# Stores and loads of split queries and latents on ScalarE's queue, and shorter due times for the mixers' steps

## The chip, the core and the metric

The kernel runs on one core of a Trainium2 chip. A core has TensorE (PE in the profile; its weight loads are the row PEld), VectorE (DVE), ScalarE (ACT), GpSimd (POOL) and SyncE (SP). Each engine runs its own list of instructions in order and waits at semaphores for the others. DMAs are begun by an engine's queue and carried out by 16 DMA engines. The metric is the time of one execution in microseconds (us).

## What is computed

One inference step of a two-layer decoder trunk, float32, over 1024 prompt tokens and 8 x 4 sampled tokens (1056 columns in all). Each layer projects its normalised input once (`x @ w_in`) and feeds three groups of heads: SSD (a Mamba-2 mixer, 16 heads of 64), MLA (latent attention, 8 heads, key/value latent 256, query rank 384, rotary keys of 32) and GDN (gated DeltaNet, 4 heads of 128). Their outputs are gated, joined and projected back, and a LayerNorm closes the layer. The sampled tokens' attention also reads 8192 cached positions through a page table. Cut to what matters here:

```python
proj = x @ w_in                                  # feeds SSD, MLA and GDN
y_ssd = rms_norm(ssd_scan(...) * silu(z))
cq  = rms_norm(mla_cq, mla_q_norm_w)             # 384 wide: the query latents
ckv = rms_norm(mla_ckv, mla_kv_norm_w)           # 256 wide: key/value latents, also an output
q = cq @ mla_w_uq                                # 8 heads x (64 + 32); the 32 are rotated
o_lat = mla_attention(q_lat, q_rope, [past, ckv], [past_rope, kr], pos)
y_gdn = rms_norm(gdn_scan(...)) * silu(z)
x = layer_norm(ALPHA * x + [y_ssd | y_mla | y_gdn] @ w_out)
```

## The kernel before

Everything lies transposed: channels on the 128 partitions, tokens along the free dimension, in three blocks of 384, 384 and 288 columns (`BLOCKS`). A float32 operand of a big product is split into a high part in a type that TensorE reads at full rate and a low part (the rest); `mm3` makes a product from high x high, high x low and low x high. `split` (L160 to L166) makes the high part with a ScalarE copy and the low part with a subtraction on GpSimd, or on VectorE where the call says so.

Each layer has two phases. In phase 1 (`phase1`) the order of TensorE's instructions is written out by `merge` (L372), a planner with a clock of its own. The clock advances by what each matmul ought to take. There are three threads of work:

- `fill`: the 46 chunks of the input projection (`proj`, three blocks each), then, when the input's tiles are given back, the queries (`mla_q`: 18 products, 6 chunks in 3 blocks), then, after stream a has ended (`yield {"a"}`), the keys and values (`mla_kv`: 16 products) with the decode queries (`absorb`) in their midst.
- stream a: `misc`, GDN heads 0 and 2, `mla_in` (it norms the key/value and query latents, splits them and stores the halves to `ckd` and `cqd` in HBM), SSD group 0.
- stream b: the first LayerNorm, GDN heads 1 and 3, `gdn_sample`, SSD group 1.

A stream's step ends in `yield t`: its next step is due when the clock has passed `t` more microseconds, and until then `fill` goes on. `yield {…}` waits until the named chunks or stages are done. The order so made is TensorE's; the other engines' and queues' orders are made by the framework's scheduler from its own estimates. The steps that the change touches:

- `rstd` (L305): column sums on TensorE, then a power of -1/2 on VectorE and GpSimd (L317, L318), `yield 5.5`, then the broadcast on TensorE. It serves `mla_in` (6 a layer), `ssd_norm` (3 for each SSD group), the first LayerNorm (three blocks in layer 0, one in layer 1), and phase 2's LayerNorms, where `finish` goes through it without waiting for due times.
- `gdn_block` (L858), two halves for each head: after the norm of its output, `yield 7.5`, then the transposes back (L150).
- `ssd` (L1031): three groups of transposes and score products, `yield 2.5` between them.
- `ssd_sample` (L1212): at a group's end, `rstd` for two prompt blocks, then eight updates of sampled states, the first due after 7.0, the others after 2.03, then the sampled y (stored to `yd`), and `ssd_norm` of the last block, which reads it back, scales it and stores it to `mixd`.

All plain DMAs are begun by SP's queue, which keeps its order (`dma`, L134 to L136, takes another engine as its last argument). Four kinds of them bear on the change: `mla_in`'s stores of halves (30 a layer, tiles `c` or `q` to `ckd`, `cqd`); `latents` (six loads `cq` from `cqd`, two for each block); `store` in `mla_q` (36 stores `qd` from `stage`); and in `absorb` eight loads of decode queries (`c` from `qxd`). The tiles `cq` lie where the input's tiles lay, those of the first block among them.

Phase 2 begins with `decode_units`: 32 units, each of which gathers cached rows with GpSimd's indirect DMAs (`dec_v`, `dec`) into room that lay in phase 1's tiles (b's region `p_b` first, then the projection's weights), transposes them on VectorE and multiplies them (`ps_dS`, `ps_dV`). The prompt's attention is woven in, then the output projection. In the profile's names, `ps_pj`, `ps_a` and `ps_b` are PSUM banks of the projection, stream a and stream b (the queries, keys and values use `ps_pj` and `ps_a` by turns); `c` and `q` are a's regions, `p_b` and `p_sb` are b's.

Of the kernel before, what the change touches and what calls it, by code (L numbers as in the profile page):

```python
# [127 lines left out]
class Builder:  # L128
# [177 lines left out]
    def rstd(self, T, tag, ss, n, mul, eps, soon=contextlib.nullcontext):  # L306

        nc = self.nc
        ws = [(j, c, min(128, n - c)) for j, c in enumerate(range(0, n, 128))]
        ps, r = self.psum(tag), T(8)  # L310
        for j, c, w in ws:
            self.mm(ps[:w, j:j + 1], lhsT=ss[:, c:c + w], rhs=self.ones[:, 0:1], start=True, stop=True)
        full = n // 128
        with soon():
            for p, u in ((128, slice(0, full)), (n % 128, slice(full, full + 1))):
                if p:
                    nc.vector.tensor_scalar(out=r[:p, u], in0=ps[:p, u], scalar1=mul, scalar2=eps, op0=ALU.mult, op1=ALU.add)  # L317
                    nc.gpsimd.tensor_tensor(out=r[:p, u], in0=r[:p, u], in1=self.mhalf[:p, 0:1].to_broadcast([p, u.stop - u.start]), op=ALU.pow)  # L318
        yield 5.5
        ps = self.psum(tag)  # L320
        for j, c, w in ws:
            self.mm(ps[:, c:c + w], lhsT=r[:w, j:j + 1].to_broadcast([w, 128]), rhs=self.ident[:w, :w], start=True, stop=True)
        return ps[:, :n]
# [385 lines left out]
    def gdn_block(self, r, L, T, Q, h, nb, x, S, ahead):  # L709
        nc = self.nc  # L710
        k, q, v, zs, g, bt = x
# [143 lines left out]
        ro = norm(po, 1.0 / 128, RMS_EPS)  # L855
        on = t(T)
        self.tt(nc.vector, v3(on), v3(po), bc(ro))
        yield 7.5  # L858
        p = tps(on)
        self.stt(on, p, self.gnwh[:, 0:1], zs)  # L860
        self.mix_out(12 + h, c0, n, on)
# [157 lines left out]
    def ssd(self, r, g):  # L1019
        nc, l = self.nc, self.l  # L1020
        R = Ring(self.reg[r][0])
        yield {-1, 17 + g * 10, 18 + g * 10}
        CT, Bt, CB, acc = R(NT), R(9 * 128), R(8 * 128 + 32), R(NT)
        X, X2 = R.rest(), Ring(self.reg[r][1])
        BT = X(NT)
        self.dma(BT, self.pd[:, 16 + g * 2])
        self.dma(CT, self.pd[:, 17 + g * 2])
        yield 13.0
        for t0 in (0, 4, 8):
            if t0:  # L1030
                yield 2.5  # L1031
            p, p2 = self.psum(r), self.psum(r)
            for t in range(t0, min(t0 + 4, 9)):
                w = 128 if t < 8 else 32
                o = (t - t0) * 128
                self.tp(p[:w, o:o + 128], BT[:, t * 128:t * 128 + w])
                self.mm(p2[:w, o:o + w], lhsT=BT[:, t * 128:t * 128 + w], rhs=CT[:, t * 128:t * 128 + w], start=True, stop=True)
            with self.tc.high_priority():
                if t0 < 8:
                    nc.scalar.copy(out=Bt[:, t0 * 128:t0 * 128 + 512], in_=p)  # L1040
                    self.tt(nc.vector, CB[:, t0 * 128:t0 * 128 + 512].rearrange("p (c n) -> p c n", c=4), p2.rearrange("p (c n) -> p c n", c=4),
                            self.const[:, C_INC:C_INC + 128].unsqueeze(1).to_broadcast([128, 4, 128]))
                else:
                    nc.scalar.copy(out=Bt[:32, 1024:1152], in_=p[:32, :128])
                    self.tt(nc.vector, CB[:32, 1024:1056], p2[:32, :32], self.const[:32, C_INCS:C_INCS + 32])

        big = self.sm(r, F32R)
        K = slice(0, 96)
        bs = X(128)
        self.stack(bs.bitcast(F32R), Bt[0:32, 1024:1152], 1)  # L1050
        self.tt(nc.gpsimd, big[K, 512:1536].rearrange("p (b n) -> p b n", b=8), bs[K].unsqueeze(1).to_broadcast([96, 8, 128]),
                self.const[K, C_BMT:C_BMT + 8].unsqueeze(2).to_broadcast([96, 8, 128]))
        for k in range(4):
            yield {19 + g * 10 + 2 * k, 20 + g * 10 + 2 * k}
            Y = Ring(X.a, X.base, X.size)
            yield from self.ssd_pair(r, Ring(Y(3 * 512)), Ring(X2.a), Ring(Y(6 * 128)), g * 4 + k, CT, Bt, CB, acc, k == 0)
        yield from self.ssd_sample(r, X, X2, g, CT, Bt, CB, acc, big)
# [95 lines left out]
    def ssd_sample(self, r, X, T, g, CT, Bt, CB, acc, big):  # L1153
# [55 lines left out]
        for b in range(8):  # L1209
            if b == 4:  # L1210
                old((6, 7))
            yield 2.03 if b else 7.0  # L1212
            p = self.psum(r)
            self.mm(p, lhsT=b3[K, b], rhs=xs[K], start=True, stop=True)
            self.tt(nc.vector, hb[b], hb[b], p, ALU.add)
            self.dma(self.o["ssd_s"][l, :, g, b], hb[b])
# [23 lines left out]
    def mla_in(self, r):  # L1240
        nc, l = self.nc, self.l
        par = self.par[l]
        a, b = self.reg[r]
        R = itertools.cycle([(Ring(a, 0, 1920), Ring(a, 1920, 2304)), (Ring(a, 4224, 1920), Ring(b))])
        yield set(range(37, 42))
        for first, cnt, pn, dst in ((39, 2, P_KVN, self.ckd), (36, 3, P_QN, self.cqd)):
            for nb, (c0, n, _) in enumerate(BLOCKS):
                T, T2 = next(R)
                raw = T(cnt * 384)[:, :cnt * n].rearrange("p (c n) -> p c n", c=cnt)
                self.dma(raw, self.pd[:, first:first + cnt, c0:c0 + n])  # L1250
                acc, sq = T(384)[:, :n], T(384)[:, :n]
                for c in range(cnt):
                    self.act(sq if c else acc, raw[:, c], AF.Square)
                    if c:
                        self.tt(nc.gpsimd, acc, acc, sq, ALU.add)
                yield 6.61
                sq = yield from self.rstd(T2, r, acc, n, 1.0 / (128 * cnt), RMS_EPS)
                for c in range(cnt):
                    self.stt(raw[:, c], raw[:, c], par[:, pn + c:pn + c + 1], sq)
                    hi, lo = (T2(384)[:, :n].bitcast(F32R) for _ in range(2))  # L1260
                    self.split(None, raw[:, c], n, hi, lo)
                    self.dma(dst[0][:, c, c0:c0 + n], hi)
                    self.dma(dst[1][:, c, c0:c0 + n], lo)
                if cnt == 2:
                    self.dma(self.o["ckvT"][l, :, :, c0:c0 + n], raw)
                    if nb == 2:
                        self.dma(self.cks, raw[:, :, 256:288])
        self.done.add("latents")

    def mla_q(self, cq, rot, ck, T):  # L1270
# [8 lines left out]
        def latents(nb):  # L1279
            c0, n, _ = BLOCKS[nb]  # L1280
            for k in range(2):
                self.dma(cq[nb][:, k], self.cqd[k][:, :, c0:c0 + n])

        banks = itertools.cycle(("pj", "a"))

# [8 lines left out]
        def store(c, nb, *q):  # L1294
            c0, n, _ = BLOCKS[nb]
            for d, a in zip(self.qd, q):
                self.dma(d[c * 128:c * 128 + 128, c0:c0 + n], a)

        def table(nb, *places):
            c0, n, _ = BLOCKS[nb]  # L1300
# [91 lines left out]
    def absorb(self):  # L1392
# [22 lines left out]
        for g in range(4):  # L1415
            G = slice(g * 32, g * 32 + 32)
            for r in range(2):
                self.dma(qx[G, r * 4:r * 4 + 4], self.qxd[:, r].rearrange("(s a) n -> a s n", s=4))
            self.dma(self.cso[G, 384:640], self.qxr)


# [608 lines left out]
```

## Time and profile before

| | |
|---|---|
| median of 3 runs | 3480.68 us (3480.07 to 3483.55) |
| the profiled execution | 3483.24 us, of which its span 3481.4 |
| TensorE busy | 3091.7 us (89% of the span), 33880 matmuls |
| VectorE busy | 2216.9 us (64%) |
| ScalarE busy | 1325.7 us (38%) |
| GpSimd busy | 1176.1 us (34%) |
| DMA | 564.70 MB in 317070 packets, mean 162 GB/s |
| phase 1, first layer | 0 to about 1051 us |
| phase 2, first layer | to about 1762 us |
| phase 1, second layer | to about 2757 us |

A row of the timeline has the start, the length, the engine, the line, the operation and its tiles (out<-in), its shape and count; in brackets stands how long the engine was idle before it and what ended that. Matmuls are pipelined and their ends modelled, so a busy TensorE isn't TensorE at its peak. A share of the whole span is a mean over stages with different limits, so the stages are read one by one.

### The profile page before, as it was taken

The numbers are of one execution on the slowest core, as the hardware profiler recorded it, in microseconds if no ns is written. First come the engines' busy times: TensorE is split into PE (matmuls) and PEld (weight loads), VectorE is DVE, ScalarE is ACT, GpSimd is POOL, SyncE is SP. The second block draws the span as 40 slices with busy tenths as digits, with TensorE's granted clock in tenths as the row PEclk, the third lists the DMA queues.
The fourth block names the chain that finished last, engine by engine and source line by source line (L and its number), as shares of the span: only waits on it lengthen the run. The fifth ranks groups of instructions, "written<-read, shape, count | busy, mean of one in ns | idle before, by whom it ended". The sixth has DMA issues, their size and how long they took to land. (4 is left out here: it accounts for less than half of the span.)

```text
span 3481.4 us, 82579 instructions
## 1 busy us (share of the span) xinstructions
PE 3091.7 (89%) x33880; PEld 2621.0 (75%) x33880; DVE 2216.9 (64%) x4610; ACT 1325.7 (38%) x3099; POOL 1176.1 (34%) x1250
## 2 busy tenths in 40 slices
PE   5899999898777888899988999989897788888997
PEld 4889998798664555569978999888886555555797
DVE  6767366577555666655687663756876456667456
ACT  4433333343222333354543332443332233334544
POOL 3444434755432212120143444455454212112100
PEclk7999999899888999999999999999998899999999
DMA  3332323556876655535434232255669656554354
GB/s 127 122 102 88 106 73 124 166 180 196 275 240 221 203 184 190 183 126 187 161 103 128 92 97 94 69 168 161 185 211 326 215 179 209 193 186 161 118 204 136
DMA packets 317070, 564.70 MB, mean 162 GB/s; under 512 B 51772, under 2 KB 218748, under 8 KB 299668
## 3 DMA queue, kind: packets, MB, share of 16 engines
q1 hardware_dynamic: 293140, 408.42, 37.1%
q0 software_dynamic: 23552, 151.01, 12.0%
q8 instruction: 266, 4.36, 0.5%
q14 instruction: 112, 0.92, 0.1%
HBM read 429.00 MB, written 130.30 MB: 161 GB/s over the span
## 5 line engine op out<-in xcount | busy, mean ns | idle before, releaser
L180 PE MATMUL ps_pj<-xh,w_r 128*128 128x384 f32 (+1 forms) x4416 | 1205.7, 340 | 65.3 <-DVE p_cv L156 29.4
L180 PEld LDWEIGHTS ps_pj<-xh,w_r 128*128 128x128 f32 x4416 | 809.7, 194 | 83.9 <-DVE p_cv L156 33.3
L180 PE MATMUL ps_pj<-xl,w_r 128*128 128x384 f32 (+1 forms) x2208 | 731.9, 331 | 5.5 <-POOL xl L153 5.4
L180 PEld LDWEIGHTS ps_pj<-xl,w_r 128*128 128x128 f32 x2208 | 429.0, 194 | 15.6 <-POOL xl L153 14.0
L156 DVE SCALAR_TENSOR_TENSOR p_cv<-p_cv,c 128x384 f32<-128x384 f32 (+1 forms) x432 | 359.5, 834 | 63.7 <-ACT p_cv L159 57.2
L180 PE MATMUL ps_dS<-dec_k,c 32*32 32x256 f32 x8192 | 332.1, 383 | 18.4 <-DVE dec_k L1704 2.1
L153 POOL TENSOR_TENSOR w_r<-w_raw,w_r 128x1024 fp32r<-128x1024 f32 (+1 forms) x98 | 235.1, 2400 | 242.8 <-ACT w_r L165 220.4
L180 PEld LDWEIGHTS ps_dS<-dec_k,c 32*32 32x32 f32 x8192 | 184.5, 106 | 144.6 <-issue 104.4
L1704 DVE STREAM_TRANSPOSE dec_k<-dec_v 128x2048 f32<-128x2048 f32 x128 | 291.0, 2281 | 0.0
L1680 POOL DMA_INDIRECT dec<-cache_k_rope,c x64 | 60.7, 949 | 523.7 <-DVE dec L1773 521.2
L159 ACT ACTIVATE c<-ps_aS,c 128x512 f32<-128x512 f32 (+3 forms) x192 | 111.2, 579 | 215.7 <-DVE c L1559 214.5
L159 ACT ACTIVATE p_cv<-p_cv 128x384 f32<-128x384 f32 x144 | 72.4, 503 | 302.7 <-DVE p_cv L156 302.2
L1680 POOL DMA_INDIRECT dec_v<-cache_kv_latent,c x128 | 120.3, 940 | 183.8 <-PE ps_dV L180 122.9
L180 PE MATMUL ps_b<-p_b 128*128 128x128 f32 (+7 forms) x1476 | 154.2, 285 | 10.5 <-DVE p_b L156 3.7
L180 PE MATMUL ps_dV<-dec_v,dec 128*32 128x256 f32 x2048 | 129.5, 395 | 37.5 <-ACT dec L1740 34.8
L180 PE MATMUL ps_aS<-mix,wo 128*128 128x384 f32 (+1 forms) x960 | 159.6, 322 | 1.4 <-DVE wo L153 1.4
L1558 DVE TENSOR_REDUCE c<-ps_aS 128x1 f32<-128x512 f32 (+3 forms) x192 | 105.3, 548 | 84.0 <-PE ps_aS L180 81.2
L1717 DVE TENSOR_REDUCE dec<-ps_dS 128x1 f32<-128x512 f32 x64 | 44.2, 691 | 179.6 <-PE ps_dS L180 179.5
L153 DVE TENSOR_TENSOR wo<-c,wo 128x1024 fp32r<-128x1024 f32 x92 | 115.4, 1254 | 67.0 <-ACT wo L165 66.6
L1515 ACT COPY c<-ps_aT 128x512 f32<-128x512 f32 (+3 forms) x192 | 89.9, 478 | 177.6 <-PE ps_aT L150 157.2
L180 PEld LDWEIGHTS ps_aS<-mix,wo 128*128 128x128 f32 x960 | 152.1, 188 | 3.6 <-DVE wo L153 2.3
L165 ACT CAST wo<-c 128x1024 fp32r<-128x1024 f32 x96 | 100.5, 1047 | 141.3 <-PE ps_aS L180 70.6
(348 smaller groups left out, 6007.3 us busy)
## 6 DMA issues: line engine op xcount, KB each, us to landing
c<-w_out SPq DMA_DIRECT2D x96, 512.0 KB
w_raw<-w_in SPq DMA_DIRECT2D x92, 512.0 KB
pd<-p_cv SPq DMA_DIRECT2D x164, 192.0 KB
p_b<-pd SPq DMA_DIRECT2D x66, 256.0 KB
c<-pd SPq DMA_DIRECT2D x64, 256.0 KB
q<-rowd SPq DMA_DIRECT2D x48, 256.0 KB
p_b<-rowd SPq DMA_DIRECT2D x48, 256.0 KB
pd<-p_cv SPq DMA_DIRECT2D x82, 144.0 KB
```

Of the source, the lines that this page charges most:

```text
L153: eng.tensor_tensor(out=out, in0=a, in1=b, op=op)
L156: self.nc.vector.scalar_tensor_tensor(out=out, in0=a, scalar=s, in1=b, op0=op0, op1=op1)
L159: self.nc.scalar.activation(out=out, in_=in_, func=func, **kw)
L165: self.nc.scalar.copy(out=hi, in_=src)
L180: return self.nc.tensor.matmul(out, lhsT=lhsT, rhs=rhs, start=start, stop=stop)
L1515: nc.scalar.copy(out=t[:, :w], in_=p[:, :w])
L1558: nc.vector.reduce_max(out=m, in_=ps[:, :w], axis=AX.X)
L1680: nc.gpsimd.indirect_dma_start(out=out, out_offset=None, in_=src, in_offset=bass.IndirectOffsetOnAxis(ap=idx[:, c:c + 1], axis=0))
L1704: nc.vector.transpose(T[r].rearrange("p j s k -> p j (s k)"), V[:, :, r * 128:r * 128 + 128])
L1717: nc.vector.tensor_reduce(out=al, in_=s3, axis=AX.XY, op=ALU.max)
```

## The change

Five due times are shortened (`rstd` 5.5 to 4.0, the end of a GDN half 7.5 to 5.5, SSD's first groups 2.5 to 1.6, the sampled states 7.0 to 4.5 and 2.03 to 1.5), and four kinds of DMA are begun by ScalarE's queue: all of `mla_in`'s split halves, of the latents' loads and of the split queries' stores, and every second pair of the decode queries' loads. No instruction is added or taken away.

```diff
@@ rstd
-        yield 5.5
+        yield 4.0
         ps = self.psum(tag)
@@ gdn_block
         self.tt(nc.vector, v3(on), v3(po), bc(ro))
-        yield 7.5
+        yield 5.5
         p = tps(on)
@@ ssd
             if t0:
-                yield 2.5
+                yield 1.6
             p, p2 = self.psum(r), self.psum(r)
@@ ssd_sample
-            yield 2.03 if b else 7.0
+            yield 1.5 if b else 4.5
             p = self.psum(r)
@@ mla_in
                     self.split(None, raw[:, c], n, hi, lo)
-                    self.dma(dst[0][:, c, c0:c0 + n], hi)
-                    self.dma(dst[1][:, c, c0:c0 + n], lo)
+                    self.dma(dst[0][:, c, c0:c0 + n], hi, nc.scalar)
+                    self.dma(dst[1][:, c, c0:c0 + n], lo, nc.scalar)
@@ mla_q, latents
             for k in range(2):
-                self.dma(cq[nb][:, k], self.cqd[k][:, :, c0:c0 + n])
+                self.dma(cq[nb][:, k], self.cqd[k][:, :, c0:c0 + n], nc.scalar)
@@ mla_q, store
             for d, a in zip(self.qd, q):
-                self.dma(d[c * 128:c * 128 + 128, c0:c0 + n], a)
+                self.dma(d[c * 128:c * 128 + 128, c0:c0 + n], a, nc.scalar)
@@ absorb
             for r in range(2):
-                self.dma(qx[G, r * 4:r * 4 + 4], self.qxd[:, r].rearrange("(s a) n -> a s n", s=4))
+                self.dma(qx[G, r * 4:r * 4 + 4], self.qxd[:, r].rearrange("(s a) n -> a s n", s=4), nc.scalar if g % 2 else nc.sync)
```

## Rows read from the trace of the kernel before

**Rows 1.** The page's first line.

```profile
span 3481.4 us, 82579 instructions
```

**Rows 2.** Windows: stretch, length, busy us of five engines, TensorE's clock, DMA share, GB/s.

```profile
570.00:921.00 351.00, 318.97 (x2307) 301.81 (x2306) 230.79 (x520) 125.42 (x266) 195.71 (x192) 0.95 0.61 188
921.00:1051.00 130.00, 87.55 (x476) 71.12 (x484) 67.97 (x142) 34.69 (x71) 45.79 (x52) 0.82 0.83 276
...
2625.00:2757.00 132.00, 89.79 (x484) 73.02 (x484) 68.39 (x138) 33.46 (x69) 46.81 (x52) 0.81 0.80 269
```

**Rows 3.** Timeline, TensorE, from the last projection to the first query products.

```profile
920.32 0.29 PE L180 MATMUL ps_pj<-xh,w_r 128*128 128x288 f32 x1
931.79 0.58 PE L180 MATMUL ps_pj<-cq,w_r 128*128 128x288 f32 x1 [11.19 <-DMA cq<-cqd]
934.34 2.29 PE L180 MATMUL ps_pj<-cq,w_r 128*128 128x288 f32 x8 [1.97 <-DMA cq<-cqd]
```

**Rows 4.** Timeline, SP's queue, at the first load of latents.

```profile
925.12 0.38 SPq L136 DMA_DIRECT2D mixd<-q  x1
925.59 0.58 SPq L136 DMA_DIRECT2D cq<-cqd  x1
```

**Rows 5.** Timeline, ScalarE, at the end of the projections.

```profile
911.52 0.49 ACT L159 ACTIVATE p_cv<-ps_pj 128x384 f32<-128x384 f32 x1 [6.77 <-PE ps_pj L180]
...
920.30 0.63 ACT L159 ACTIVATE p_b<-p_b 128x512 f32<-128x512 f32 x1 [6.57 <-DVE p_b L1108]
```

**Rows 6.** Timeline, TensorE, from the last query product to the first decode product.

```profile
980.04 3.07 PE L180 MATMUL ps_a<-cq,w_r 128*128 128x384 f32 x9 [2.64 <-DVE q L153]
...
990.70 0.27 PE L180 MATMUL ps_a<-c,c 128*32 128x1 f32 x2 [3.14 <-DVE c L1234]
992.12 0.76 PE L180 MATMUL ps_b<-p_sb 96*128 96x512 f32 x1 [1.15 <-DVE p_sb L153]
992.68 1.62 PE L180 MATMUL ps_a<-c,c 128*128 128x128 f32 x6
...
1030.15 0.65 PE L180 MATMUL ps_b<-c,p_b 128*128 128x1 f32 x6
...
1050.63 1.11 PE L180 MATMUL ps_dS<-dec,c 32*32 32x256 f32 x16 [17.69 <-issue]
```

**Rows 7.** The chain of waits, end of the second layer's phase 1: start, length, what.

```profile
2731.46 2.09 PE ps_b L180 x24
...
2735.16 1.39 PE ps_a L180 x6
...
2737.23 4.03 DMA p_b<-yd
...
2743.30 1.82 DMA mixd<-p_b
...
2748.60 6.79 DMA dec<-cache_k_rope,c
```

**Rows 8.** Timeline, TensorE: four steps behind due times that the change shortens.

```profile
318.57 1.47 PE L150 MATMUL ps_b<-c,p_b 128*128 128x128 f32 x12
...
361.59 0.60 PE L150 MATMUL ps_a<-c,q 128*128 128x128 f32 x4
...
580.29 0.83 PE L180 MATMUL ps_a<-c,c 128*128 128x128 f32 x6
...
734.30 0.49 PE L180 MATMUL ps_b<-p_b 128*128 128x128 f32 x2 [1.64 <-ACT p_b L1040]
```

**Rows 9.** Timeline, VectorE and GpSimd: what the first three steps need.

```profile
316.75 0.68 DVE L153 TENSOR_TENSOR p_b<-ps_b,p_sb 128x512 f32<-128x512 f32 x1
...
355.05 0.69 DVE L153 TENSOR_TENSOR q<-ps_a,p_sa 128x512 f32<-128x512 f32 x1
...
574.60 0.86 POOL L318 TENSOR_TENSOR c<-c,c 128x3 f32<-128x3 f32 x1
```

**Rows 10.** Waits of SP's queue, 921 to 1051: waiter, releaser, us, times, longest.

```profile
SPq L136 <- DVE stage L153: 5.3, 5, 3.8
```

**Rows 11.** The split queries by tile: issues, ns min/median/max, first and last start.

```profile
L136 SPq DMA_DIRECT2D qd<-stage x72: 319/403/2110, 945.0 to 2696.5; - x72
```

## The prediction

> **What bounds the kernel now.** I read the table of windows first, because a share over the whole span [rows 1] hides the stages. While the projections run, TensorE is the bound or close to it (319.0 of 351 us busy). In the stage behind them, from the last projection to the first decode product, it is busy for 87.6 of 130 us at a granted clock of 0.82, and the second layer repeats this: 89.8 of 132 us at 0.81 [rows 2]. Those two stretches are where time lies open, 42 us in each layer. Nothing in the change touches phase 2 itself: `rstd` runs there too, but `finish` throws its delays away.
>
> I then read TensorE's timeline of that stage for the rows that begin with a wait. They fall in three clusters.
>
> First, right behind the last projection (920.6) TensorE waits 11.19 us for the first half of the split query latents, and 1.97 us more for the second [rows 3]. The reader should ask why that load is late, not how long it takes. It goes into the room of the input's first block. ScalarE evacuates that block's last bank from 911.52 on [rows 5], so the input tiles below it are free then. The load is issued at 925.59, 14 us later, in SP's order behind a mixer's store that waited for VectorE [rows 4]. It lands 6.2 us after its issue, when TensorE starts at 931.79.
>
> Second, the queries' products end at 983.1 (980.04 and 3.07 us), but `fill` may not go on to keys and values before stream a has ended. So a's last steps stand alone in the order and TensorE waits for them: 2.64 us (a bank that a's state update still held), 3.14 and 1.15 us, 6.9 in all. The products that may follow begin when a's last `rstd` is through [rows 6].
>
> Third, the products of keys and values end by 1030.15, where b's last norm begins, and the first decode product comes at 1050.63, 20.5 us later [rows 6]. The chain of waits in the second layer says what that is: stream b's step that makes its last y ends at 2733.55; y is stored, read back for the norm (4.03 us), scaled, stored to the mix (1.82 us), and only then does b's region come free for the gathers of the cache, of which the key part lands at 2755.39 [rows 7]. That is 21.8 us of latency behind b's step, 18.8 behind the last product of keys and values (2736.55).
>
> **The change part by part.** Two things are changed: due times in the planner that orders TensorE, and the queue of 76 DMAs in each layer.
>
> *Due times.* Shorter ones move no work away. They move a stream's step forward in an order that the projections fill. For stream b the steps ahead of its last y lose 4 x 2.0 (GDN halves) + 2 x 0.9 (SSD's start) + 2 x 1.5 (norms) + 2.5 + 7 x 0.53 (sampled states) = 19.0 us of due time. For stream a the sampled part alone loses 9.2 + 1.5 = 10.7, and the steps ahead of it 6 x 1.5 + 8.0 + 1.8 = 18.8, of which some is lost again because its pairs wait for their projections.
>
> - Second cluster: a ends at 994.3 (992.68 and 1.62 us), and must end 11.2 us earlier, at 983.1, to be out of the way. 10.7 and a part of 18.8 suffice, so a's steps lie under products and the 6.9 us go. Ends: 3 (a bank wait stays) and 6.9. I take 6.9.
> - Third cluster: b's step now ends 3.0 us ahead of the last product of keys and values [rows 7]. It moves forward by 19.0, while those products move forward by the 6.9 just counted, so by some 12 against them, and it ends 15 us ahead. The key part would land 21.8 - 15 = 6.8 us after them in place of 18.8, a gain of 12; I take 11, since due times are the planner's microseconds and not the chip's. What is late next is the same chain, shorter. Ends: 0 (the gathers wait for something else of the old region) and 18.8.
> - What it may cost: a step due before its operands are ready stalls TensorE, which keeps its order, and every projection behind it. `rstd`: GpSimd is ready at 575.46, the product comes at 580.29, 4.8 us of room for 1.5. A GDN half: VectorE ready at 355.74, transposes at 361.59, 5.9 us for 2.0; the tightest has 317.43 to 318.57, 1.1 for 2.0, so 0.9 lost [rows 8, 9]. SSD's start already waits 1.64 us for a bank in stream b [rows 8]; two steps there come 0.9 sooner, so 1.8 lost. The sampled states: nothing, up to the rival below. Sum 2.7 a layer; ends 0 and 5.
>
> *Queue.* The 30 stores of split latents and 36 of split queries, six loads of latents and four of the decode queries leave SP. What stays on SP behind them (weights, rows, states) waits for fewer strangers; I cost that at nothing, as none of the three clusters waits for such a load.
>
> - The latents' loads: on ScalarE's queue they no longer stand behind b's store, but ScalarE keeps order too. In this trace an exponential blocks it from 913.7 (the end of the one before) to 920.30 [rows 5]. Ahead of that, the load goes out at 912 and TensorE waits for nothing (gain 13.2, the sum of the two waits). Behind it, it goes out at about 921, lands at 927 and gains 4.6 and most of the second wait, 6. Behind everything, 0. I take 7: with b's steps earlier the exponential stands elsewhere, and I can't tell where.
> - The stores: each now costs ScalarE an issue, 0.40 us in the median as SP's rows have it and 2.11 at most [rows 11], and a wait for the low part. On SP, waits for VectorE's low parts were 5.3 us in this stage, 3.8 the longest [rows 10]. Behind a waiting store on ScalarE stand casts that empty PSUM banks, and behind those TensorE. With about half its time idle here (34.7 of 130 us busy [rows 2]) I let half of the 5.3 reach TensorE: 2.7 a layer. Ends: below nothing by the SP relief, say -2, and 40 (below).
> - The decode queries' loads: four of eight elsewhere; nothing, they end before the decode's start as it will be.
>
> The page "DMA: Bandwidth & Descriptors" of the Trainium skill, section "Issuing engines are not separate DMA queues", speaks against this half: it says that starting DMAs from several engines saves only the sequencer's time to start them. Here a row shows a load that could have gone 14 us earlier and was held by the order of its queue, which is more than an issue; by the page's rule the loads' term is 0 and the time is that of the first rival.
>
> **Sum.** A layer: 7 + 6.9 + 11 - 2.7 - 2.7 = 19.5 us, two layers 39. The profiled execution took 3483.2 (span 3481.4), the median is 3480.7 (3480.1 to 3483.6), so the sum is 3444.2 on the profiled one and **3442** as a median. I add nothing for a clock that falls less after shorter waits; if it comes, it is a gain.
>
> **The rivals.**
>
> - *The queue is worth nothing*: the loads wait on ScalarE as long as on SP. For it: ScalarE also keeps order, and its exponential waits for a row load of SP's. Against: the tiles are free at 911.5. Net 6.9 + 11 - 2.7 - 2.7 = 12.5 a layer: 3456.
> - *All three clusters close*: 13.2 + 6.9 + 18.8 - 2.7 = 36.2 a layer: 3408. Against it: the chain of rows 7 doesn't get shorter itself.
> - *New waits of TensorE take it back*: some 40 steps a layer are due earlier (8 GDN halves, 12 norms, 4 SSD starts, 16 states). At 0.5 us of wait for each, 20 us, the gain is gone: about 3481. For it: the rows at 318.57 and 734.30; against it: the rooms of 4.8 and 5.9.
> - *Slower: ScalarE becomes the bound of the query stage.* Place: 18 products with two stores each, from 931.8 to 983.1, one in 2.85 us. ScalarE needs a cast, 0.49 by the nearest row of that size [rows 5], and two issues, 0.81; it has 1.55 us left for the wait of each product. Beyond that point each product is late. If each waited the 3.8 us that SP's longest took, 18 x 2.25 = 40 us a layer: 22.2 - 40 = -18 a layer, 3517. For it: nothing else empties those banks; against it: five such waits in the stage, 1.1 us in the mean [rows 10].
>
> **How the numbers follow.** Forecast 0.45 (3430 to 3455); queue worth nothing 0.2; all close 0.1; new waits 0.13, of which 0.08 lies within 0.2%; slower 0.12. 0.2% is 7 us, about what a measurement of this kernel can tell from no change. Faster 0.80, same 0.08, slower 0.12. The range takes in the first two, most of the third and the nearer part of the fourth: 3410 to 3478.
>
> **What would show it.** After: the latents' loads issued by ScalarE, TensorE's wait behind the last projection 2 to 7 us and not 13; no wait between the last query product and the first of keys and values, with a's last norm ahead of them; the first decode product 7 to 12 us behind the last of keys and values, not 20.5; the windows of projections the same within 10 us, as a few us of the streams' work move into them; the query stage's products no farther apart than 2.85 us. I am wrong if the query stage is longer with ScalarE waiting for VectorE's low parts, if projections wait more often for mixers' steps, or if the gathers are released by something other than b's region.

## The result and the profile after

The changed kernel took 3526.0 us (median of 4 runs, 3518.3 to 3530.2) against 3482.1 of the kernel before (4 runs, 3480.1 to 3487.2): ratio 1.0121, 95% interval 1.0100 to 1.0142. The forecast was 3442, its range 3410 to 3478. The profiled execution took 3530.15, its span is 3528.0 against 3481.4 [rows 1].

The stages first, cut at the first and the last projection product and at the first decode product of each layer (stretch, length, busy us of TensorE, its weight loads, VectorE, ScalarE, GpSimd, TensorE's clock, DMA share, GB/s). Before:

```profile
36.00:920.60 884.60, 810.76 (x7286) 761.40 (x7286) 585.89 (x1187) 327.79 (x795) 429.30 (x458) 0.95 0.42 131
920.60:1050.60 130.00, 87.18 (x469) 70.87 (x468) 67.97 (x143) 35.09 (x72) 45.52 (x51) 0.82 0.83 276
1765.80:2624.20 858.40, 797.00 (x7258) 754.30 (x7258) 573.82 (x1167) 315.48 (x766) 416.28 (x443) 0.97 0.42 133
2624.20:2756.40 132.20, 89.23 (x472) 72.82 (x473) 68.59 (x139) 34.26 (x71) 46.23 (x52) 0.81 0.80 269
```

After:

```profile
36.00:968.80 932.80, 838.02 (x7384) 784.14 (x7384) 609.32 (x1235) 335.11 (x808) 443.76 (x475) 0.94 0.42 133
968.80:1072.70 103.90, 76.80 (x373) 65.39 (x372) 49.49 (x94) 29.94 (x58) 30.16 (x36) 0.81 0.77 267
1785.70:2694.40 908.70, 824.08 (x7356) 777.69 (x7357) 594.87 (x1209) 321.86 (x778) 432.42 (x459) 0.95 0.43 134
2694.40:2799.50 105.10, 77.85 (x373) 65.97 (x371) 49.67 (x98) 29.50 (x58) 30.76 (x36) 0.79 0.78 266
```

The tail, from the last projection to the first decode product, is 26.1 and 27.1 us shorter, and the projections are 48 and 50 us longer. Not all of the tail's gain is waiting saved. In layer 0, 96 products moved from the tail into the projections and took 10.4 us of TensorE with them (87.18 to 76.80); TensorE's idle time in the tail fell by 15.7 us (42.8 to 27.1; 43.0 to 27.3 in layer 1), where the forecast's terms for the tail make 22.2. Among the projections TensorE's idle time grew by 21 us (884.6 - 810.8 = 74 to 932.8 - 838.0 = 95); with the 10.4 us of moved products that leaves some 17 us, which is the same products taking longer at a lower granted clock (0.95 to 0.94).

TensorE's timeline of the tail, rows that answer to [rows 3] and [rows 6]:

```profile
975.55 0.58 PE L180 MATMUL ps_pj<-cq,w_r 128*128 128x288 f32 x1 [5.63 <-DMA cq<-cqd]
...
977.14 2.29 PE L180 MATMUL ps_pj<-cq,w_r 128*128 128x288 f32 x8 [1.01 <-DMA cq<-cqd]
...
984.31 2.84 PE L180 MATMUL ps_pj<-cq,w_r 128*128 128x384 f32 x8 [2.06 <-DMA cq<-cqd]
...
1018.21 2.98 PE L180 MATMUL ps_pj<-cq,w_r 128*128 128x384 f32 x9 [3.79 <-DVE stage L153]
...
1060.71 1.56 PE L180 MATMUL ps_a<-w_r,ck 128*128 128x512 f32 x6
1072.72 1.11 PE L180 MATMUL ps_dS<-dec,c 32*32 32x256 f32 x16 [10.46 <-issue]
```

All three clusters shrank: the latents' 13.16 us to 8.70 (11.49 to 9.36 in layer 1), a's 6.9 us to nothing, the decode's 17.69 to 10.46. The 8.70 is 6.64 behind the last projection and a third wait of 2.06 us, for the next block's latents, that the kernel before doesn't have. Four other waits stand in the query stage, 3.79 us the longest. Among the projections the largest new waits are these:

```profile
630.41 0.63 PE L150 MATMUL ps_b<-c,p_b 32*128 32x32 f32 x4 [9.22 <-DVE p_b L153]
...
680.44 0.79 PE L180 MATMUL ps_a<-c 128*128 128x128 f32 x2 [6.44 <-DVE c L153]
...
689.05 0.45 PE L150 MATMUL ps_b<-c,p_b 128*128 128x128 f32 x1 [4.38 <-DVE p_b L991]
...
942.66 0.76 PE L180 MATMUL ps_a<-p_sa 96*128 96x512 f32 x1 [5.64 <-DVE p_sa L153]
```

Two of the four are shortened steps, an SSD group of a's (680.44) and a's first sampled state (942.66). The other two belong to the sampled GDN, whose own due times nobody touched. To name a place, count the projection chunks (72 products each, 46 a layer) that TensorE has done. From 30 to 33 chunks its waits in layer 0 grew from 7.0 to 22.4 us, from 33 to 35 they fell from 6.9 to 1.5, from 35 to 39 they grew from 1.9 to 11.5, and from 44 to 46 from 4.2 to 7.7; layer 1 has the same places.

### The profile page after: what moved, and what is told of

Same layout as the page of the kernel before. It is cut to its first block, busy times and chain, and to the rows that moved or that the text cites. A ratio compares the mean times of both kernels' runs of the same rounds, so it can differ in the third digit from the quotient of the medians.

```text
span 3528.0 us, 82535 instructions
## 1 busy us (share of the span) xinstructions
PE 3125.2 (89%) x33880; PEld 2656.2 (75%) x33880; DVE 2223.2 (63%) x4610; ACT 1329.7 (38%) x3099; POOL 1174.2 (33%) x1250
## 5 line engine op out<-in xcount | busy, mean ns | idle before, releaser
L180 PE MATMUL ps_pj<-xh,w_r 128*128 128x384 f32 (+1 forms) x4416 | 1228.2, 345 | 53.6 <-DVE p_cv L156 19.8
L180 PEld LDWEIGHTS ps_pj<-xh,w_r 128*128 128x128 f32 x4416 | 825.8, 198 | 71.3 <-DVE p_cv L156 23.1
L180 PE MATMUL ps_pj<-xl,w_r 128*128 128x384 f32 (+1 forms) x2208 | 739.6, 335 | 7.1 <-POOL xl L153 7.1
L180 PEld LDWEIGHTS ps_pj<-xl,w_r 128*128 128x128 f32 x2208 | 437.4, 198 | 17.0 <-POOL xl L153 14.2
L156 DVE SCALAR_TENSOR_TENSOR p_cv<-p_cv,c 128x384 f32<-128x384 f32 (+1 forms) x432 | 349.8, 811 | 81.1 <-ACT p_cv L159 75.1
L153 POOL TENSOR_TENSOR w_r<-w_raw,w_r 128x1024 fp32r<-128x1024 f32 (+1 forms) x98 | 231.6, 2363 | 249.9 <-ACT w_r L165 228.3
L180 PEld LDWEIGHTS ps_b<-p_b 128*128 128x128 f32 (+5 forms) x1476 | 136.1, 164 | 40.4 <-DVE p_b L156 15.2
L153 DVE TENSOR_TENSOR wo<-c,wo 128x1024 fp32r<-128x1024 f32 x92 | 115.4, 1254 | 64.7 <-ACT wo L165 64.4
L165 ACT CAST wo<-c 128x1024 fp32r<-128x1024 f32 x96 | 100.5, 1047 | 144.7 <-PE ps_aS L180 69.5
```

The costliest lines, as they stand in the source:

```text
L153: eng.tensor_tensor(out=out, in0=a, in1=b, op=op)
L156: self.nc.vector.scalar_tensor_tensor(out=out, in0=a, scalar=s, in1=b, op0=op0, op1=op1)
L165: self.nc.scalar.copy(out=hi, in_=src)
L180: return self.nc.tensor.matmul(out, lhsT=lhsT, rhs=rhs, start=start, stop=stop)
```

## The experiments

Two numbers locate each kernel's time: how much longer its projections are than before's (first to last projection product), and its tail (130.0 and 132.2 us before). A third turned out to matter: how far stream b's SSD blocks stand behind stream a's, read from the trace at the four transposes that open a block, in projection chunks (72 products) that TensorE has done by then, over chunks 38 to 44. The last column is TensorE's wait for a projection bank that VectorE had not emptied (p_cv), in chunks 38 to 46. Pairs are layers 0 and 1; differences are worked out from the traces, one for each kernel.

| kernel | ratio to before, 95% | projections, us longer | tail, us | b behind a, chunks | wait for p_cv, us |
|---|---|---|---|---|---|
| before | 1 | 0, 0 | 130.0, 132.2 | 0.54 to 0.62 | 5.0, 4.8 |
| changed | 1.0121 (1.0100 to 1.0142) | 48.0, 50.3 | 103.9, 105.1 | 0.5 to 0.76, one gap | 2.0, 3.6 |
| e1_due | 1.0007 (0.9993 to 1.0021) | 33.1, 40.2 | 95.3, 96.2 | as changed | 1.5, 2.3 |
| e2_dma | 1.0024 (1.0009 to 1.0039) | -2.7, 0.8 | 135.3, 136.0 | as before | 5.5, 5.3 |
| e3_samp | 0.9993 (0.9978 to 1.0008) | -2.3, -0.6 | 130.5, 131.5 | as before | 6.0, 6.4 |
| e4_gdn | 1.0136 (1.0110 to 1.0163) | 33.3, 35.6 | 124.3, 118.7 | 0.0 to 0.09 | 18.7, 17.6 |
| e5_nogdn | 1.0090 (1.0069 to 1.0111) | 20.9, 20.5 | 126.8, 128.2 | 0.0 to 0.09 | 22.5, 20.0 |
| e6_due_qd | 1.0041 (1.0027 to 1.0056) | 41.1, 38.6 | 100.6, 101.8 | as changed | 2.2, 0.0 |
| e7_due_min | 1.0052 (1.0032 to 1.0072) | 43.4, 49.0 | 94.9, 96.8 | as changed | 2.7, 0.8 |
| e8_back | 1.0121 (1.0101 to 1.0140) | 16.1, 26.0 | 130.1, 122.6 | 0.0 to 0.17 | 16.9, 14.3 |
| e9_gdn65 | 1.0009 (0.9996 to 1.0021) | 15.6, 15.7 | 117.2, 117.6 | 0.50 to 0.62 | 7.3, 8.1 |
| e10_gdn95 | 0.9962 (0.9947 to 0.9977) | -14.7, -19.5 | 137.8, 145.9 | 0.54 to 0.71 | 4.7, 3.5 |
| e11_rstd | 1.0075 (1.0054 to 1.0096) | 15.5, 17.9 | 129.0, 129.9 | 0.0 to 0.13 | 16.7, 16.0 |
| e12_ssd | 0.9913 (0.9893 to 0.9933) | -7.9, -4.9 | 121.8, 122.8 | 0.50 to 0.59 | 3.1, 2.6 |
| e13_rstd_a18 | 1.0012 (0.9998 to 1.0026) | -2.1, 2.2 | 134.7, 129.6 | 0.54 to 0.62 | 4.6, 6.6 |
| e14_a20 | 1.0184 (1.0161 to 1.0207) | 21.4, 21.3 | 139.8, 144.7 | 0.0 to 0.12 | 22.3, 20.5 |
| e15_ssd_gdn95 | 0.9974 (0.9960 to 0.9989) | -8.1, -8.3 | 133.5, 136.1 | 0.54 to 0.63 | 3.2, 2.6 |
| e16_due_a30 | 0.9985 (0.9971 to 1.0000) | 17.7, 17.1 | 109.6, 111.7 | 0.54 to 0.71 | 4.2, 5.3 |

Each ratio is against the kernel before on the same chip. For e5 to e8 and e13 to e16 that took 3394 to 3395 us in place of 3482 to 3485: phase 2 is shorter on those chips (the first layer's takes 665 to 670 us in every kernel run there, 711 to 715 in every other), the stages of phase 1 that an edit leaves alone are not (e14_a20 and before are within 0.5 us of each other through layer 0's first 34 chunks), so the columns of phase 1 can be compared.

**The halves of the change.** e1_due is the first four hunks of the diff, e2_dma the other four.

> The changed kernel without its queue half: all five due times shortened, every DMA on SP's queue. Theory D (the due times put mixers' steps ahead of their operands, and TensorE waits there in the middle of the projections, 48 to 50 us a layer): those stay, the 6.6 us that the latents' load gained in each layer go, 3530 to 3545. Theory Q (ScalarE, stopped by the 66 stores a layer that it now begins, is late with casts, VectorE after it, and the mixers' steps after that): the projections are as before and the tail gains its 14 to 20 us a layer, 3440 to 3460.

> The queue half alone: four kinds of DMA begun by ScalarE, due times as before. Theory D: the latents' wait shrinks by about 6.6 us a layer and little else changes, 3462 to 3475. Theory Q: the projections lose 40 us or more a layer, 3520 to 3560.

Each half alone comes out near the kernel before, and neither theory has it. The due times do all that the tail gains (35 and 36 us) and lose 33 and 40 us in the projections. The windows of e1_due, cut as above, show what that is:

```profile
36.00:953.40 917.40, 826.36 (x7384) 772.74 (x7383) 606.27 (x1231) 334.65 (x807) 443.91 (x475) 0.95 0.43 134
953.40:1048.70 95.30, 71.90 (x377) 61.91 (x377) 48.67 (x99) 29.68 (x58) 31.16 (x36) 0.84 0.87 296
1760.80:2659.50 898.70, 817.93 (x7356) 772.57 (x7357) 596.73 (x1206) 321.23 (x779) 432.58 (x460) 0.95 0.43 135
2659.50:2755.70 96.20, 72.54 (x376) 62.53 (x379) 48.37 (x100) 29.53 (x58) 30.97 (x36) 0.84 0.86 293
```

TensorE's idle time fell by 19.4 and 19.3 us in the tail and grew by 17.2 and 19.4 us among the projections. The waits changed their place; the rest is 15 and 17 us of products that moved with them.

The DMAs cost 5 and 4 us in the tail on their own; on top of the due times, the changed kernel less e1_due, they cost 15 and 10 us in the projections and 9 and 9 in the tail, 43 us in both layers. (By the medians the two kernels are 42 us apart, 3526.0 and 3484.3.) Some 15 of the 43 are idle time of TensorE; some 28 are the same products taking longer at a lower granted clock (0.948 to 0.935 and 0.953 to 0.946 in the projections, 0.84 to 0.81 and 0.79 in the tail). The latents' wait, that part's only purpose, is 7.40 us with every load on SP (6.79 in layer 1):

```profile
961.18 0.58 PE L180 MATMUL ps_pj<-cq,w_r 128*128 128x288 f32 x1 [6.69 <-DMA cq<-cqd]
...
962.47 0.85 PE L180 MATMUL ps_pj<-cq,w_r 128*128 128x288 f32 x2 [0.71 <-DMA cq<-cqd]
```

The changed kernel's ScalarE shows why its queue is no better: the load stands behind the evacuation of the last projection's bank, so it can't go out before that projection (which ends at 968.84):

```profile
968.88 0.41 ACT L159 ACTIVATE p_cv<-ps_pj 128x288 f32<-128x288 f32 x1 [4.88 <-PE ps_pj L180]
968.89 0.62 ACTq L136 DMA_DIRECT2D cq<-cqd  x1
```

The load goes out right behind the last projection and lands 6.7 us later, when TensorE starts (975.55). With the third wait counted, ScalarE's queue made the latents' wait longer on top of the due times, 8.70 against 7.40 and 9.36 against 6.79 us. With the due times as before (e2_dma) it made it shorter by little, 11.57 against 13.16 and 10.46 against 11.49.

The page "DMA: Bandwidth & Descriptors" of the Trainium skill, section "Issuing engines are not separate DMA queues", says that another issuing engine saves only the time of starting a DMA. The trace agrees: no gain here is above 1.6 us.

**The stores, one kind at a time**, on e1_due. Edits:

```diff
 e6_due_qd, mla_q, store
-                self.dma(d[c * 128:c * 128 + 128, c0:c0 + n], a)
+                self.dma(d[c * 128:c * 128 + 128, c0:c0 + n], a, nc.scalar)
 e7_due_min, mla_in
-                    self.dma(dst[0][:, c, c0:c0 + n], hi)
-                    self.dma(dst[1][:, c, c0:c0 + n], lo)
+                    self.dma(dst[0][:, c, c0:c0 + n], hi, nc.scalar)
+                    self.dma(dst[1][:, c, c0:c0 + n], lo, nc.scalar)
```

> All five due times shortened, and of the DMAs the split queries' stores alone begun by ScalarE. With all due times and every DMA on SP the query stage took 42 us (961.2 to 1003.4), in the changed kernel 52 (975.5 to 1027.9). Theory S (ScalarE, held by each store's wait for its low part, sets the query stage's pace): the stage is 50 us or more, about 10 us a layer, 3500 to 3512. Rival (the stores are harmless, the other DMAs cost it): 3480 to 3490, the stage 42 to 45.

> All five due times shortened, and of the DMAs the 30 stores of normed latents a layer alone begun by ScalarE. Theory M (these stores hold ScalarE in the middle of the projections, whose chunks 31 to 46 took 15 and 10 us longer in the changed kernel than with every DMA on SP): projections 10 us a layer longer, query stage 42 to 45 us, 3500 to 3512. Rival (they cost nothing, and what the projections lost came from elsewhere): 3480 to 3490.

Both theories held in place; S missed in size (48 us, where it had 50 or more, and a ratio that makes 3496 where it had 3500 to 3512). The windows of the query stage, same 200 products each, of e1_due, e6_due_qd and the changed kernel:

```profile
961.20:1003.40 42.20, 36.77 (x200) 33.09 (x201) 27.98 (x53) 13.53 (x28) 16.50 (x21) 0.90 0.96 350
2666.60:2709.90 43.30, 37.48 (x200) 33.67 (x201) 27.91 (x53) 13.39 (x28) 16.47 (x21) 0.89 0.96 349
```

```profile
968.80:1017.10 48.30, 38.86 (x200) 34.44 (x201) 27.03 (x52) 12.16 (x26) 15.17 (x21) 0.83 0.90 325
2631.80:2680.10 48.30, 38.10 (x200) 33.99 (x201) 26.68 (x52) 12.15 (x26) 15.24 (x21) 0.84 0.89 321
```

```profile
975.50:1027.90 52.40, 41.60 (x200) 36.73 (x201) 30.16 (x53) 12.74 (x27) 15.59 (x21) 0.82 0.82 297
2701.90:2753.90 52.00, 42.64 (x200) 37.69 (x201) 28.55 (x52) 12.15 (x26) 16.23 (x21) 0.78 0.80 291
```

The split queries' stores cost that stage 6 and 5 us, all four kinds 10 and 9. TensorE at a lower clock makes 2.1 and 0.6 us of the former and about half of the latter. In e6_due_qd the largest part is one wait of stream b's first sampled state, 5.50 us where e1_due has 0.47 (6.30 and 0.47 in layer 1). GpSimd has the step's operand ready at 988.37, but ScalarE casts it 4.1 us later, behind casts and stores of queries:

```profile
991.07 1.34 ACTq L136 DMA_DIRECT2D qd<-stage  x3
992.46 0.62 ACT L173 CAST p_sb<-p_b 32x512 fp32r<-32x512 f32 x1 [1.10 <-DVE q L156]
```

```profile
994.51 0.77 PE L180 MATMUL ps_b<-p_sb 96*128 96x512 f32 x1 [5.50 <-DVE p_sb L153]
```

The latents' stores leave the query stage alone (40.5 and 43.0 us) and cost the projections 10 and 9 us over e1_due, 8 and 9 of them by the time 33 chunks are done; they are issued from 27 to 32. The waits of TensorE from 600 to 720 us, e1_due and then e7_due_min (waiter, releaser, us, times, longest):

```profile
PE ps_b L150 <- DVE p_b L153: 0.6, 1, 0.6
```

```profile
PE ps_b L150 <- DVE p_b L153: 10.4, 2, 8.9
```

That is the changed kernel's 9.22 us. Its ScalarE, some 15 us ahead of it, is held by four stores in a row, with the bank's evacuation behind them:

```profile
613.51 2.63 ACTq L136 DMA_DIRECT2D cqd<-q  x4
616.25 0.49 ACT L159 ACTIVATE p_cv<-ps_pj 128x384 f32<-128x384 f32 x1 [2.28 <-DMA cqd<-q]
```

That the stores' engine makes the wait is shown; the links between these two rows and the wait are not. The loads' own share of the 43 us, some 6 by difference, was not run alone either.

**The due times, one at a time.**

```diff
 e3_samp
-            yield 2.03 if b else 7.0
+            yield 1.5 if b else 4.5
 e4_gdn (e9_gdn65: 6.5, e10_gdn95: 9.5)
-        yield 7.5
+        yield 5.5
 e11_rstd
-        yield 5.5
+        yield 4.0
 e12_ssd
-                yield 2.5
+                yield 1.6
```

e5_nogdn is e3_samp, e11_rstd and e12_ssd together.

> One due time alone: the sampled states' (7.0 and 2.03 to 4.5 and 1.5), DMAs on SP. These steps stand at the end of stream a's and b's last mixers. Theory D: a's last waits (6.9 us a layer) and a part of the decode's wait (up to 7 us) close and the projections lose under 5 us a layer, 3455 to 3475. Theory Q says the same or better: 3450 to 3465. A third theory, that these 16 steps are what stalls TensorE: 3490 or more.

> One due time alone: the end of a GDN half (7.5 to 5.5), DMAs on SP. The projections' first growth in the changed kernel (chunks 13 to 17, 10 us) and its largest (chunks 30 to 33, 16 us) lie at the GDN heads and the sampled GDN. Theory D: about half the loss is here, 3495 to 3520. Theory Q: within 5 us of before, 3476 to 3487.

> The due times of the norms, of SSD's first groups and of the sampled states shortened, the GDN half's left at 7.5; DMAs on SP. Theory G (the loss in the projections belongs to the GDN half's due time alone): projections within 8 us a layer of before, the tail (130 and 132 us from the last projection to the first decode product) 5 to 15 us shorter, 3455 to 3475. Rival (every shortened step costs its share): projections 15 us a layer longer, 3480 to 3500.

e3_samp changed nothing, not even the tail. e4_gdn lost as much as the whole change, and e5_nogdn, the rest without it, lost 0.9%. So the parts don't add: GDN +1.36% and the rest +0.9%, together +0.07%. Theory G fell.

> The GDN half's due time alone, half as far: 7.5 to 6.5, DMAs on SP. With 5.5 the time was 47 us above the kernel before on the same chip, 50 of it in the two first phases. Theory E (every us that later steps stand earlier is a us of wait, the room of the operands being used up): half of that, 15 to 30 us above the kernel before. Theory F (the kernel before stands in a place where TensorE's order and the orders of VectorE, GpSimd and SP happen to fit, and any other order costs about the same): 35 to 55 us above it, as with 5.5.

> The GDN half's due time alone, lengthened: 7.5 to 9.5, DMAs on SP. Theory E (earlier steps wait for operands, later ones don't): TensorE's idle time within the projections is the same or up to 5 us a layer less, the tail 5 to 10 us a layer longer, in all 0 to 20 us above the kernel before. Theory F (any other order than that of the kernel before costs): the projections take 15 us a layer more, 30 to 60 us above the kernel before.

> The norms' due time alone: 5.5 to 4.0, DMAs on SP. The norms' room was 2.4 to 6.2 us where 1.5 are taken. Norms, SSD's groups and sampled states together were 31 us above the kernel before, the sampled states alone 0. Theory N (the norms shift SSD's stage and that costs the whole): 25 to 35 us above. Rival (SSD's own due time does it): within 8 us of the kernel before.

> The due time of SSD's first groups alone: 2.5 to 1.6, DMAs on SP. In the kernel before one of these steps waited 1.64 us for its bank. Theory N: within 8 us of the kernel before, the steps' own waits of about 1 us each. Rival (these steps, two for each group, cost the whole of the 31 us of norms, SSD's groups and sampled states together): 25 to 35 us above it.

Theory F fell: two single edits beat the kernel before, e12_ssd by 0.87% (0.67 to 1.07), the best of all kernels here. Theory N had the norms' size and missed SSD, which gained. The GDN due time of 9.5, 7.5, 6.5 and 5.5 gives projections of -15, 0, +16 and +33 us in layer 0, so theory E has that column, though neither total: the tail pays most of the first three back (138, 130, 117 us) and little of the last (124).

**Putting the later steps back.**

```diff
 e8_back, on e4_gdn, end of gdn_block
         self.mix_out(12 + h, c0, n, on)
+        yield 1.4
         return S
```

> The GDN half's due time alone shortened (7.5 to 5.5), and behind its last step a due time of 1.4 added, which puts the sampled GDN and what follows it back where they stood in TensorE's order of the kernel before (the step of 4 32x32 products of that stage stands at chunk 31.08, as before; with 5.5 alone it stood at 30.42). Theory P (the shortened step itself waits for nothing; the loss comes from the later stages, which then stand earlier against the loads and against VectorE's work for SSD): 3476 to 3492. Rival (the shortened step stalls TensorE): 3510 to 3530 as with 5.5 alone.

Neither: when 33 chunks are done, this kernel stands 3.2 us ahead of the kernel before in layer 0 and level with it in layer 1 (e4_gdn: 18.5 and 19.8 behind), so the shortened steps themselves cost nothing; but the loss came back in the next chunk and in chunks 40 to 46. What e4, e5, e8 and e11 share is the column "b behind a": there both streams open their SSD blocks at once.

**The offset of the streams, tested by itself.** One line, in `ssd`:

```diff
 e13_rstd_a18, on e11_rstd (e14_a20, on before: 20.0; e16_due_a30, on e1_due: 30.0)
-        yield 13.0
+        yield 18.0 if r == "a" else 13.0
```

> The norms' due time 4.0 as in the run with norms alone (27 us above the kernel before), and stream a's first SSD step due after 18.0 in place of 13.0, which puts its blocks back to 0.54 of a chunk from b's. Theory Ph (the two streams' SSD blocks fall on VectorE together and the projections' banks are emptied late): the projections are within 5 us a layer of the kernel before, the time within 10 us of it, 15 to 30 us less than with the norms alone. Rival (the norms' steps themselves wait): 20 to 30 us above the kernel before, as without the 18.0.

> The kernel before with one due time lengthened: stream a's first SSD step is due after 20.0 in place of 13.0, which puts its blocks onto b's (both at chunks 38.75, 39.96 and 40.08, 41.29). No step stands earlier. Theory Ph: the projections lose 15 to 20 us a layer, most of it in chunks 40 to 46, 25 to 45 us above the kernel before. Rival (only steps that stand earlier wait): the projections lose nothing, the time is 0 to 12 us above.

Theory Ph held in both. With the norms as short as in e11_rstd, moving a's blocks back to half a chunk from b's took the loss away (1.0075 to 1.0012, projections 16 to -2 us). With no step earlier than before, moving a's blocks onto b's cost 1.8%, more than any part of the change and more than expected: 21 us a layer in the projections, of which 17 and 16 are waits for a projection bank, and 10 and 13 in the tail, where a, due 7 us later, ends later. The rows: where blocks open before (a, then b) and in e14_a20 (both):

```profile
779.37 0.60 PE L150 MATMUL ps_a<-c,c 128*128 128x128 f32 x4
...
798.54 0.60 PE L150 MATMUL ps_b<-c,p_b 128*128 128x128 f32 x4
```

```profile
838.66 0.60 PE L150 MATMUL ps_a<-c,c 128*128 128x128 f32 x4
...
839.09 0.60 PE L150 MATMUL ps_b<-c,p_b 128*128 128x128 f32 x4
```

and what that makes of VectorE, TensorE and GpSimd in e14_a20, some 10 us earlier, behind the blocks opened before these:

```profile
823.34 0.68 DVE L1108 TENSOR_SCALAR q<-q,c 128x128 f32<-128x128 f32 x3 [3.76 <-DMA q<-rowd]
...
826.63 2.25 DVE L1108 TENSOR_SCALAR p_b<-p_b,c 128x128 f32<-128x128 f32 x2
828.80 1.76 DVE L153 TENSOR_TENSOR q<-q,c 128x512 f32<-128x512 f32 x1
830.49 1.25 DVE L1108 TENSOR_SCALAR p_b<-p_b,c 128x128 f32<-128x128 f32 x6
...
832.26 0.54 DVE L156 SCALAR_TENSOR_TENSOR p_cv<-p_cv,ps_pj 128x384 f32<-128x384 f32 x1
```

```profile
832.86 0.69 PE L180 MATMUL ps_pj<-xh,w_r 128*128 128x384 f32 x1 [7.92 <-DVE p_cv L156]
```

```profile
826.00 1.57 POOL L153 TENSOR_TENSOR p_b<-p_b 128x384 f32<-128x384 f32 x1 [5.00 <-DVE p_b L153]
827.54 1.26 POOL L153 TENSOR_TENSOR q<-q,c 128x512 f32<-128x512 f32 x1
828.76 1.25 POOL L153 TENSOR_TENSOR c<-c,q 128x512 f32<-128x512 f32 x1
```

VectorE waits for a's rows, does work of a's block (`q`) and of b's (`p_b`) by turns, and only then reads the projection's bank; TensorE has waited 7.92 us for it. The rows of 2.25 us (two instructions) and 1.76 us are stretched: in the kernel before such instructions take 0.28 and 0.68 us each where no GpSimd product runs, and here GpSimd's products for both blocks do (last section). From chunk 35 on, VectorE is busy for 167.0 us in place of 154.9 in layer 0, with 374 instructions in place of 380, and its row steps (L1108) take 462 ns in the mean in place of 352. So by these rows blocks that coincide cost twice: VectorE has two at a time, and each is slowed by the other's GpSimd products. How much of the 21 us each makes was not tested apart.

The wait column parts the kernels without exception: 14 to 23 us a layer where the blocks coincide, 0 to 8 where they don't. The changed kernel and e1_due are among the latter, with less of this wait than the kernel before: what they lose in the projections is not this. Their new waits stand from 30 to 33 and from 35 to 39 chunks.

> The two single changes that gained, together: SSD's first groups 2.5 to 1.6 (30 us below the kernel before) and the GDN half 7.5 to 9.5 (13 us below). b's SSD blocks stand 0.55 of a chunk from a's. Theory Ph with sums: 30 to 45 us below the kernel before. Rival (a shift of one part changes what the other is worth, so that gains don't add): between 12 us below and 15 above.

> All five due times shortened, every DMA on SP (within 5 us of the kernel before), and stream a's first SSD step due after 30.0 in place of 13.0: a's first block then stands at chunk 34.6 in place of 33.1, behind the end of b's sampled GDN, its blocks 0.6 of a chunk from b's, and its last step still ahead of the last query products. Theory Ph: the 12.5 us wait at chunk 33 and part of the growth in chunks 35 to 39 go, the tail keeps its 35 us a layer, 15 to 40 us below the kernel before. Rival (the wait moves to the next place): within 8 us of it.

Two gains don't add here either: e15_ssd_gdn95 keeps 0.26% of 1.25, its tail 134 and 136 us in place of e12_ssd's 122 and 123, as its rival said. e16_due_a30's time is also the rival's. Its theory was right about chunks 35 on (projections 15 and 23 us shorter than e1_due's) and wrong about chunk 33, where the wait stayed; a's end, 17 us of due time later, gave 14 and 16 us of tail back. VectorE's and TensorE's rows there suggest what holds it: a's first row work (`q`), slowed by GpSimd's products beside it, runs long ahead of its due time, between two steps of b's sampled GDN:

```profile
658.81 5.94 DVE L1108 TENSOR_SCALAR q<-q,c 128x128 f32<-128x128 f32 x8 [2.25 <-DMA q<-rowd]
...
665.34 1.22 DVE L996 COPY p_b<-p_b 32x128 f32<-32x128 f32 x4
```

```profile
673.37 0.79 PE L180 MATMUL ps_b<-p_sb 96*128 96x512 f32 x1 [10.76 <-POOL p_sb L153]
```

Due times order TensorE alone; VectorE's order is the scheduler's. That removing this row work from its place would close the wait was not tried.

## Why the prediction was wrong, step by step

- *Second cluster, 6.9*: right, gone in both layers.
- *Third cluster, 11 (0 to 18.8)*: right in direction; TensorE's wait fell by 7.2, and the decode starts 10.45 us behind the last product of keys and values, inside the 7 to 12 named. But what is late next is not "the same chain, shorter". Stream b is out of the chain, the sign named for being wrong: in the changed kernel's second layer the gathers start half a us behind the last but one group of products of keys and values, and their key part lands 7.59 us after its own start. The chain there:

```profile
2786.36 1.41 PE ps_pj L180 x6
...
2788.30 1.11 POOL dec_v L1680
...
2790.95 7.59 DMA dec<-cache_k_rope,c
```

- *The latents' loads, 7*: 4.5 and 2.1 us came (13.16 to 8.70, 11.49 to 9.36), and not by the queue. With SP's queue and short due times the gain is 5.8 and 4.7 (e1_due); ScalarE's queue alone is worth 1.6 and 1.0 (e2_dma), and less than nothing on top of the due times. ScalarE's order holds the load until the last projection, the branch that the prediction priced at 0. Two readings behind this term were weak: no single store held SP's queue (from 908 to 927 it waited at most 1.3 us at a time, mostly for DMAs, with others to issue in between), and that the room is free at 911.5 no run shows: the earliest issue in any kernel here is 1.7 us ahead of the last projection's end (e5_nogdn).
- *Stores, 2.7*: failed. Alone on top of the due times the two kinds of stores cost 17 us (e6_due_qd) and 19 us (e7_due_min) in two layers, projections and tail over e1_due's, against 5.4 forecast. The prediction looked at SP's waits for low parts in the tail [rows 10] and at the query stage alone; the latents' stores run 300 to 400 us earlier, where ScalarE empties the banks of the projections, and no row of ScalarE there was read. The slower rival had its place right, and e6_due_qd measured its price: 6 and 5 us, not 40. The clock, put at nothing or a gain, fell, and makes some 28 of the 43 us that the queue half cost.
- *New stalls, 2.7 (0 to 5)*: this step failed most. e1_due has 33 and 40 us: 17 and 19 of idle time, 15 and 17 of products that left the tail, the rest dearer products. The idle time alone takes back all that the tail's waits gave. The room of 4.8, 5.9 and 1.1 us [rows 8, 9] was measured at the shortened step, in the order of before, and for the sampled states, put at nothing, no row was read (a's first waits 5.64 us in the changed kernel). e8_back shows that the GDN steps have their room; what has not is what a step pushes: every later step of its stream stands earlier, by sums that differ between streams (the six norms of `mla_in` are a's alone), and so meets the other stream's work, the rows' loads and the banks at another time. For the norms' due time alone, e13_rstd_a18 shows it: the offset put back, the loss is gone. For all due times together the places of the waits are known, not their causes.
- *The rivals* were priced as if one excluded the next. "New waits take it back", 20 us a layer, is e1_due: 17 and 19 us of waits, 3481.2 profiled, 3481 forecast. Its reason was not: the waits are not 0.5 us at each of 40 steps but a few of 2 to 12.5 us, some at steps that nobody shortened, so the close number is partly luck. The change is that rival with the stores' cost on top, a case the prediction did not write down.

Open: the waits from 30 to 33 chunks in the kernels with shorter GDN steps (20.0 us in one wait in e4_gdn, 12.5 in e1_due) were read from rows, not tested, and with them the cause of most of what the due times lose in the changed kernel; and why the tail gives 35 us with all due times and at most 15 with any one is a sum of shifts that was not taken apart.

## What to carry to other kernels

Where two hand-ordered streams share an in-order engine, read the offset between their heavy stretches before pricing a due time: moving one stream onto the other cost 1.8% with no step made earlier, and an offset of half a chunk cut a loss of 0.75% to 0.12%. Room at the changed step says what that step costs, not what its followers will meet; read the rows of every stage that shifts, and price cases together. When work moves from one stage to another, compare idle time stage by stage, not the stages' lengths. A store that waits is not free on an engine that empties another engine's banks, however idle that engine is on the mean.

## What the hardware showed

VectorE's row step (L1108, 128x128) is there 256 times in the kernel before. Where it began with no GpSimd product (L153) running, it took 278 ns in the mean (231 of them, 271 to 289). The 25 that began while one ran took 1147 ns in the mean, up to 2464, and every one of them ended 80 to 86 ns behind the end of that product, whatever its length. In e1_due, with GpSimd's four products from 653.11 to 660.89 and without:

```profile
657.46 4.69 DVE L1108 TENSOR_SCALAR q<-q,c 128x128 f32<-128x128 f32 x8 [1.84 <-DMA q<-rowd]
...
663.98 1.69 DVE L1108 TENSOR_SCALAR p_b<-p_b,c 128x128 f32<-128x128 f32 x8
```

The page "Trainium Architecture — The Big Picture" of the Trainium skill, section "What this means for kernel authors", says that VectorE and GpSimd share a port pair and lock each other out; these rows agree. The chips differ too: the kernel before took 3394 to 3395 us on two of them, 2.5% less than on the others, and the traces of the kernels run there put it in phase 2 (665 to 670 us in the first layer against 711 to 715).
